# The opening of a decoder layer's kernel: split weights not kept in DRAM, the second group's x through the first one's tiles, the first weight tile in four parts, another order of splits

## The chip, the cores and the metric

One core of one Trainium2 chip runs the whole layer. The metric is the device time of one execution in microseconds; a kernel's time is the median of its runs. The kernel before takes 2134.07 us (three runs, 2131.14 to 2137.16).

## The reference

A decoder layer for 2048 tokens of 1024 features, with 16 meta tokens ahead of them. All of it is float32.

```python
xn = rms_norm(h, norm_gain[l])
proj = xn @ w_in[l]
sb_q, sb_k, sb_v, sw_q, sw_k, sw_v, sb_z, sw_z, g_sb, g_sw = jnp.split(proj, offsets, axis=-1)
o_sb = stick_breaking_attention(sb_q, sb_k, sb_v, valid)          # 8 heads of 64
q = rope(sw_q, pos); k = rope(sw_k, pos)
o_sw = sliding_window_sink_attention(q, k, sw_v, attn_sinks[l], valid)   # 16 query, 2 key heads, window 128
y_sb = (o_sb * jax.nn.silu(sb_z)) @ w_branch_sb[l]
y_sw = (o_sw * jax.nn.silu(sw_z)) @ w_branch_swa[l]
merged = jax.nn.sigmoid(g_sb) * y_sb + jax.nn.sigmoid(g_sw) * y_sw
h = h + merged @ w_out[l]
```

The shapes of heads are left out above. What matters here is the second line: one product of the normalised x with w_in, whose columns are the queries, keys, values and gates of both branches.

## The kernel before

**Split products.** TensorE multiplies operands of a narrower kind, so every float32 operand is split in two: h, its rounded copy, and l, the rest. A product is three products, h by h, l by h and h by l. `gemm` (L409 to L411) does this for one column tile of 128 columns and one group of 512 tokens: eight k slices of 128 features, three matmuls of 128x512 each, 24 in all. `gemm_meta` (L420) is the same for the 16 meta tokens, 16 small matmuls. The x operands are xh and xl, the weight operands wh and wl.

**Weights.** `weights` (L164 to L183) brings a column tile: it loads 512 KB into `raw` (two buffers), and `split` makes wh (ACT, L106, or POOL, L108) and wl (DVE or POOL, L109), with three buffers of each. It then stores both halves in DRAM (`kept`), 512 KB each, so that a later use loads wh and wl and splits nothing. In the opening these stores are collected in `put_off` and issued in two lots of six.

**Groups and halves.** The 2048 tokens are four groups of 512, worked on in two halves, groups 2 and 3 first. In the first half g0 is group 2 and g1 is group 3. The program's second half uses weight tiles that the opening had.

**The opening** (L970 to L1123) is what the change is about. ACT, SP and DVE work through its instructions in the order in which the code gives them; SP issues all DMAs. Behind it, up to `hand.close()`, DVE's order still is the code's; the rest is set by the scheduler. TensorE's order is the code's throughout. The opening goes so:

1. The first column tile, SBK0 (keys of the stick-breaking branch), and eight tiles of g0's x are loaded. x is not normalised yet: `unscaled` (L979, L980) multiplies a k slice by the gain alone and splits it. `by_halves` (L1017, L1021) splits the weight tile in two halves. Products of three column tiles (SBK0, SBQ0, SBK1; the tiles `sbt[:3]` are given in another order) run from this for g0 and g1 while the sums of squares are made.
2. Meanwhile g0's x is scaled: `normal` (L382 DVE, L383 ACT, L385 DVE) multiplies a slice by gain and row scale, casts it to xh and subtracts to xl. SWK and SWV (keys and values of the window branch) are loaded and split, and the row products of the three tiles are scaled out of PSUM (`scaled`, L1002 on DVE), then split by `evac_split` (L112 ACT, L113 DVE) and stored as kd (keys) and qd (queries), with h and l in tiles of the pool `tmp` (seven buffers).
3. g1's x is loaded a second time and scaled by `normal`. Four of its slices go to the pool `xs` (four buffers, `ring_x`), two into a buffer of `raw`, and the last two to `xs` again, which is only free when the first pair has been split. `normal` for g1 stands behind the `evac_split` of g1.

**Behind the opening** the window's products run: SWK, SWV and the first query tile SWQ0 for g0, then SWK and SWV for g1 with their meta tokens, then SWQ0 for g1 and more query tiles. `rope` (L637 to L641) turns SWK's product, with the tables ct and sn (512 KB each, one DMA each). `put_k` (L649 ACT, L651 DVE) splits it into kk, four DVE operations; `put_q` (L699) does this for queries. SWV's product is copied out (L484), turned by four transposes on TensorE (L488) into a PSUM bank, `zm`, that has one buffer, and split into vv (L112, L113).

Of the kernel before, what the change touches and what calls it, by code (L numbers as in the profile page):

```python
# [16 lines left out]
P = 128  # L17
# [4 lines left out]
GT = 512  # L22
# [17 lines left out]
def f32(ap):  # L40
    return ap.bitcast(F32)
# [3 lines left out]
def tile_kernel(ctx, tc, x, xt, meta, metat, gain, w_in, w_sb, w_sw, w_out, sinks, fgain,  # L45
# [55 lines left out]
    vsplit, hsplit = [False], [True]  # L101
# [349 lines left out]

    def low(acc):
# [517 lines left out]
    with (tc.tile_pool(name="start", bufs=1, side="left") as bp,  # L970
          tc.manual_schedule(engines={mybir.EngineType.Activation, mybir.EngineType.SP})):
        hsplit[0] = vsplit[0] = True
        raws, accs, ms = [], {}, [None] * 3

        def unscaled(g, k, t):

            DMA(t, xt[g, k])
# [37 lines left out]
        def by_halves(wh, wl, raw):  # L1015
            a, b = slice(0, KT // 2), slice(KT // 2, KT)
            A.copy(wh[:, a], raw[:, a])  # L1017
            V.tensor_tensor(wl[:, a], raw[:, a], f32(wh[:, a]), op=ALU.subtract)

            def rest():  # L1020
                A.copy(wh[:, b], raw[:, b])  # L1021
                G.tensor_tensor(wl[:, b], raw[:, b], f32(wh[:, b]), op=ALU.subtract)
            second.append(rest)
# [232 lines left out]
```

## Time and profile before

| what | value |
|---|---|
| median of three runs | 2134.07 us (2131.14 to 2137.16) |
| the profiled execution | 2136.89 us |
| its span in the trace | 2135.0 us |
| mean granted TensorE clock | 0.997 |
| DMA packets | 174519, 380.39 MB, mean 178 GB/s |
| stores of split weights | 50 of h and 50 of l, 512 KB each |
| loads of split weights | 66 of wh and 66 of wl, 512 KB each |
| loads of raw w_in tiles | 50, 512 KB each |

How to read the rows that the next sections show. Times are microseconds from the span's start. A timeline row has start, duration, engine, line, operation and tiles (out<-in), how many instructions of the kind stand together, and in brackets the idle time before with the engine or DMA that ended it. A row of waits has the engine, the tile and line that waited, whom for, and the total, the number and the longest wait. A row of windows has, for a stretch, each engine's busy time with its instruction count, then the granted clock (1.00 is full speed), the mean busy share of the 16 DMA engines and their GB/s. PE is TensorE's matmul, PEld its weight load, DVE VectorE, ACT ScalarE, POOL GpSimd, SP the queue that issues DMAs.

### The profile page before, as it was taken

To read this page: it belongs to the slowest core of one execution; us is meant where nothing else is said; L and a number is where in the kernel's file an instruction comes from. 1 tells how busy PE (TensorE), PEld (TensorE's weight loads), DVE (VectorE), ACT (ScalarE), POOL (GpSimd) and SP (SyncE) were. 2 spreads that over 40 slices of the span, in tenths; PEclk is the share of its full clock that TensorE was granted. 3 is DMA by queue.
4 is the path that set the end of the run, shared out by engine and by line. 5 is a ranking of instruction groups with operands and counts; after the bars stand their busy time and mean duration, and the time that the engine had idled before them with its cause. 6 is when DMAs were issued, how large, how long until landed. Compare 5 with 4: busy or idle time off the path is not lost.

```text
span 2135.0 us, 30157 instructions
## 1 busy us (share of the span) xinstructions
PE 2112.2 (99%) x10534; PEld 1755.9 (82%) x10534; DVE 1383.4 (65%) x2158; ACT 1030.5 (48%) x2471; POOL 333.1 (16%) x453
## 2 busy tenths in 40 slices
PE   8999999999999999999999999999999999999998
PEld 6788888888888788888888888888888888887887
DVE  7797885466555443867746888888885446553453
ACT  6677774344444434777744565555554202221121
POOL 2122332332232300122210000000000232000000
PEclk9999999999999999999999999999999999999999
DMA  9855455766556464443465333323423986557432
GB/s 334 289 182 194 173 177 175 233 219 208 183 184 204 151 221 159 157 157 139 138 196 165 121 123 118 120 97 112 119 85 132 346 297 198 192 216 270 157 110 79
DMA packets 174519, 380.39 MB, mean 178 GB/s; under 512 B 22720, under 2 KB 40960, under 8 KB 174368
## 3 DMA queue, kind: packets, MB, share of 16 engines
q1 hardware_dynamic: 174368, 378.48, 52.5%
q8 instruction: 83, 1.36, 0.3%
q14 instruction: 68, 0.56, 0.1%
HBM read 237.35 MB, written 140.98 MB: 177 GB/s over the span
## 4 chain that ended last, share of the span: by engine, by line
PE 85%; issue 7%; DMA 3%; DVE 2%; ACT 1%; SPq 1%; POOL 0%; POOLq 0%; DVEq 0%; ACTq 0%
PE ps_g L409 15%; PE ps_g L411 14%; PE ps_g L410 14%; PE ps_o L927 5%; PE ps_t L896 4%; PE ps_z L876 4%; PE ps_z L718 3%; PE ps_o L764 3%; PE ps_g L232 1%; PE ps_g L233 1%; PE ps_z L231 1%; PE ps_z L233 1%; PE ps_z L232 1%; PE ps_g L231 1%; PE ps_t L747 1%
## 5 line engine op out<-in xcount | busy, mean ns | idle before, releaser
L409 PE MATMUL ps_g<-xh,wh 128*128 128x512 f32 x1544 | 634.6, 411 | 7.0 <-ACT xh L979 7.0
L410 PE MATMUL ps_g<-xl,wh 128*128 128x512 f32 x1544 | 605.9, 392 | 0.0
L411 PE MATMUL ps_g<-xh,wl 128*128 128x512 f32 x1544 | 605.9, 392 | 0.0
L883 DVE TENSOR_TENSOR_SCAN row<-row 128x512 f32<-128x512 f32 (+2 forms) x320 | 375.6, 1175 | 157.9 <-POOL row L881 105.8
L411 PEld LDWEIGHTS ps_g<-xh,wl 128*128 128x128 f32 x1544 | 290.2, 188 | 65.5 <-DVE wl L109 0.3
L409 PEld LDWEIGHTS ps_g<-xh,wh 128*128 128x128 f32 x1544 | 291.3, 189 | 52.7 <-ACT xh L979 7.0
L410 PEld LDWEIGHTS ps_g<-xl,wh 128*128 128x128 f32 x1544 | 292.0, 189 | 43.2 <-DVE xl L980 1.3
L879 ACT ACTIVATE row<-ps_z 128x512 f32<-128x512 f32 (+2 forms) x320 | 165.0, 516 | 192.0 <-PE ps_z L876 191.3
L113 DVE SCALAR_TENSOR_TENSOR wtl<-ps_t,wth 128x512 fp32r<-128x512 f32 (+1 forms) x320 | 189.9, 594 | 55.7 <-ACT wth L112 54.9
L112 ACT ACTIVATE wth<-ps_t 128x512 fp32r<-128x512 f32 (+1 forms) x320 | 170.5, 533 | 71.8 <-PE ps_t L896 68.9
L876 PE MATMUL ps_z<-kt,q 128*128 128x512 f32 (+4 forms) x640 | 178.2, 353 | 0.0
L896 PE MATMUL ps_t<-ident,row 128*128 128x128 f32 x1088 | 171.1, 272 | 1.9 <-DVE wtl L113 1.2
L896 PEld LDWEIGHTS ps_t<-ident,row 128*128 128x128 f32 x1088 | 135.7, 140 | 39.1 <-DVE wtl L113 2.3
L881 POOL TENSOR_SCALAR_AFFINE_SELECT row<-row 128x128 f32<-128x128 f32 x128 | 42.0, 329 | 630.1 <-ACT row L879 591.0
L876 PEld LDWEIGHTS ps_z<-kt,q 128*128 128x128 f32 x640 | 118.9, 188 | 23.2
L927 PE MATMUL ps_o<-wth,vc 128*128 128x512 f32 (+1 forms) x320 | 125.1, 391 | 0.0
L108 POOL TENSOR_SCALAR wh<-raw 128x1024 fp32r<-128x1024 f32 (+1 forms) x63 | 68.2, 1082 | 336.1 <-PE ps_g L410 209.5
L726 ACT ACTIVATE sc<-sc,nm 128x129 f32<-128x129 f32 x256 | 100.2, 394 | 41.7 <-DVE nm L724 40.9
L927 PE MATMUL ps_o<-wtl,vc 128*128 128x512 f32 (+1 forms) x320 | 116.9, 365 | 0.7 <-DVE wtl L113 0.7
L577 ACT ACTIVATE tmp<-ps_g 128x512 f32<-128x512 f32 x112 | 67.0, 599 | 103.9 <-PE ps_g L411 97.5
L109 POOL TENSOR_TENSOR wl<-raw,wh 128x1024 fp32r<-128x1024 f32 (+1 forms) x43 | 100.5, 2337 | 3.3
L270 ACT CAST ringl<-gt 128x512 fp32r<-128x512 f32 x32 | 20.0, 624 | 152.3 <-DVE gt L268 144.6
(316 smaller groups left out, 3439.2 us busy)
## 6 DMA issues: line engine op xcount, KB each, us to landing
wh<-h_in_w_in SPq DMA_DIRECT2D x66, 512.0 KB, 3.6
wl<-l_in_w_in SPq DMA_DIRECT2D x66, 512.0 KB, 4.9
raw<-in_w_in SPq DMA_DIRECT2D x50, 512.0 KB, 5.1
h_in_w_in<-wh SPq DMA_DIRECT2D x50, 512.0 KB, 2.9
l_in_w_in<-wl SPq DMA_DIRECT2D x50, 512.0 KB, 2.9
q<-qd SPq DMA_DIRECT2D x128, 128.0 KB, 3.1
vc<-vd SPq DMA_DIRECT2D x48, 256.0 KB, 3.3
kd<-tmp SPq DMA_DIRECT2D x32, 256.0 KB, 3.9
```

Source lines behind the costliest of these rows:

```text
L109: (V if vsplit[0] else G).tensor_tensor(l, src, f32(h), op=ALU.subtract)
L112: A.activation(h, acc, AF.Copy, scale=scale)
L113: V.scalar_tensor_tensor(l, acc, scale, f32(h), op0=ALU.mult, op1=ALU.subtract)
L409: T.matmul(acc, lhsT=wh[:, k, :], rhs=xh[g][:, k, :], start=k == 0, stop=False)
L410: T.matmul(acc, lhsT=wh[:, k, :], rhs=xl[g][:, k, :], start=False, stop=False)
L411: T.matmul(acc, lhsT=wl[:, k, :], rhs=xh[g][:, k, :], start=False, stop=k == KT - 1)
L726: A.activation(sc[:, hh, :], sc[:, hh, :], AF.Exp, bias=nm[:, hh:hh + 1], accum_out=den[:, hh:hh + 1])
L876: T.matmul(acc[:, :b - a], lhsT=lq, rhs=kt[h][:, k0 + a:k0 + b], start=t == 0, stop=t == 1)
L879: A.activation(r[:, a:b], acc[:, :b - a], AF.Sigmoid, scale=-1.0)
L883: V.tensor_tensor_scan(r[:, :w], r[:, :w], r[:, :w], last[j] if n else 1.0, op0=ALU.mult, op1=ALU.min)
L896: T.transpose(tr[:, j * P:(j + 1) * P], rows_of[h, g, n - (j > i), j][:, k0:k0 + P], ident)
L927: T.matmul(o[:, :n], lhsT=v, rhs=r, start=first and r is wh, stop=last and r is wl)
```

## The change

It edits the opening and what goes with it:

- The six column tiles that are split in the opening (SBK0, SBQ0, SBK1, SWK, SWV, SWQ0) are no longer stored to DRAM, neither there nor later. Each later use loads the raw tile and splits it again.
- The first weight tile is loaded in four DMAs of 128 KB (two k slices each), between those of x, and split in four parts. The gain comes transposed by the host, so that a partition's eight values lie together.
- All eight slices of g1's second x are loaded, behind SWQ0's raw tile, into the eight tiles `raw0` that held g0's first x.
- `normal` for g1 stands ahead of g1's `evac_split`.
- The h halves of keys and queries go to `xs` where `spare` says that they may.

The diff, cut to its core:

```diff
-        kept[key] = [dram(f"{t}_{w.name}_{c0}", [P, n, P], F32R) for t in "hl"]
-        for t, k in zip((wh, wl), kept[key]):
-            if put_off is None:
+        if opening[0]:
+            loose.append(key)
+        elif key not in loose:
+            kept[key] = [dram(f"{t}_{w.name}_{c0}", [P, n, P], F32R) for t in "hl"]
+            for t, k in zip((wh, wl), kept[key]):
                 DMA(k, t)
-            else:
-                put_off.append((k, t))
...
+    def high():
+        return ring_x(F32R) if spare[0] else tmp(F32R)
...
-            h, l = tmp(F32R), low(acc)
+            h, l = high(), low(acc)
...
+        def by_parts(wh, wl, raw):
+            def part(a, b, e):
+                A.copy(wh[:, a:b], raw[:, a:b])
+                e.tensor_tensor(wl[:, a:b], raw[:, a:b], f32(wh[:, a:b]), op=ALU.subtract)
+            second.append(part)
...
-        raw = load(C_SBK)
-        DMA(gn, gain.rearrange("o (k p) -> p (o k)", p=P))
-        ready[C_SBK] = weights(C_SBK, raw=raw, split=by_halves)
+        DMA(*parts[0])
+        DMA(gn, gain)
+        DMA(raws[0], xt[g0, 0])
+        DMA(raws[1], xt[g0, 1])
+        for k in range(2, KT, 2):
+            DMA(*parts[k // 2])
+            for j in (k, k + 1):
+                DMA(raws[j], xt[g0, j])
+        ready[C_SBK] = weights(C_SBK, raw=raw, split=by_parts)
...
-        for k, t in put_off:
-            DMA(k, t)
-        del put_off[:]
...
-        for k in range(4):
-            new.append(ring_x())
-            DMA(new[k], xt[g1, k])
         raw = load(C_SWQ)
-        pair = wp.tile([P, KT, P], F32, tag="raw", name="raw", bufs=2).rearrange("p k c -> p (k c)")
-        for k in (4, 5):
-            new.append(pair[:, (k - 4) * GT:(k - 3) * GT])
+        for k in range(KT):
+            new.append(bp.tile([P, GT], F32, tag="raw0", name="raw0", bufs=KT))
             DMA(new[k], xt[g1, k])
...
         for n in range(3):
             outs[g1, n] = scaled(g1, n, rb1)
+        for k in range(0, KT, 2):
+            in_turns(*(normal(g1, j, new[j], rb1) for j in (k, k + 1)))
         for n in range(3):
             ts[n][1](g1, outs[g1, n], None)
...
-        for k in range(0, KT, 2):
-            in_turns(*(normal(g1, j, new[j], rb1) for j in (k, k + 1)))
-            if k == 0:
-                for j in (6, 7):
-                    new.append(ring_x())
-                    DMA(new[j], xt[g1, j])
-                for j, t in put_off:
-                    DMA(j, t)
...
-        "gain": a["norm_gain"],
+        "gain": a["norm_gain"].reshape(KT, P).T,
```

Lines move a little: L382, L383 and L385 become L385, L386 and L388; L409 to L411 become L412 to L414; L420 becomes L423, L427 L430, L488 L495, L639 to L641 become L646 to L648, L649 and L651 become L656 and L658, L699 L706, and L1002 L1010.

TensorE's instructions stand in the same order as before. On DVE, before, from the scaling of the last unscaled product on (ps_t; L113 are the splits of g1's keys and queries, L382 and L385 are `normal` of g1):

```order
L1002 TENSOR_TENSOR tmp<-ps_t,rb 128x512
L113 SCALAR_TENSOR_TENSOR tmp<-tmp 128x512 x3
L382 SCALAR_TENSOR_TENSOR xs<-xs,gn,rb 128x512 x2
L385 TENSOR_TENSOR xl<-xs,xh 128x512 x2
L382 SCALAR_TENSOR_TENSOR xs<-xs,gn,rb 128x512 x2
L385 TENSOR_TENSOR xl<-xs,xh 128x512 x2
```

And now, at the same place (raw_733 and so on are the `raw0` tiles with g1's x; the pairs of 737, 739, 741 and 743 between are of the same form):

```order
L1010 TENSOR_TENSOR tmp<-ps_t,rb 128x512
L385 SCALAR_TENSOR_TENSOR raw_733<-raw_733,gn,rb 128x512
L385 SCALAR_TENSOR_TENSOR raw_735<-raw_735,gn,rb 128x512
L388 TENSOR_TENSOR xl<-raw_733,xh 128x512
L388 TENSOR_TENSOR xl<-raw_735,xh 128x512
...
L388 TENSOR_TENSOR xl<-raw_745,xh 128x512
L388 TENSOR_TENSOR xl<-raw_747,xh 128x512
L113 SCALAR_TENSOR_TENSOR tmp<-tmp,xs 128x512 x3
```

The three splits have moved behind the four pairs. Next on DVE, before, the rope of SWK for g0 and g1, up to the split of the first transposes of SWV:

```order
L639 SCALAR_TENSOR_TENSOR tmp<-ps_g,ct 128x512
L640 TENSOR_TENSOR tmp<-tmp,sn 128x512
L641 TENSOR_TENSOR tmp<-tmp 128x512
L639 SCALAR_TENSOR_TENSOR tmp<-ps_z,ct 128x512
L640 TENSOR_TENSOR tmp<-tmp,sn 128x512
L641 TENSOR_TENSOR tmp<-tmp 128x512
L651 TENSOR_TENSOR kk<-tmp,kk 64x512 x4
L699 TENSOR_TENSOR q<-tmp,q 64x512 x2
L113 SCALAR_TENSOR_TENSOR vv<-ps_zm,vv 128x8x64
```

(ps_g is SWK's product for g0, ps_z SWQ0's.) And now:

```order
L646 SCALAR_TENSOR_TENSOR tmp<-ps_g,ct 128x512
L109 TENSOR_TENSOR wl<-raw,wh 128x1024
L647 TENSOR_TENSOR tmp<-tmp,sn 128x512
L648 TENSOR_TENSOR tmp<-tmp 128x512
L646 SCALAR_TENSOR_TENSOR tmp<-ps_z,ct 128x512
L647 TENSOR_TENSOR tmp<-tmp,sn 128x512
L648 TENSOR_TENSOR tmp<-tmp 128x512
L658 TENSOR_TENSOR kk<-tmp,kk 64x512 x4
L109 TENSOR_TENSOR wl<-raw,wh 128x1024
L706 TENSOR_TENSOR q<-tmp,q 64x512 x2
L113 SCALAR_TENSOR_TENSOR vv<-ps_zm,vv 128x8x64
```

Two weight splits have come in between: that of the next value tile, and the second one of SWQ0. On SP's queue, before, around the tables (ct, sn; kd_2 and kd_3 are keys of g0 and g1, the number behind it names the tile):

```order
L55 DMA kd_2_101<-tmp 128x512 x2
L55 DMA ct<-in_cost 128x1024
L55 DMA sn<-in_sint 128x1024
L55 DMA raw<-in_w_in 128x1024
L55 DMA kd_3_98<-tmp 128x512 x2
L55 DMA qd_3_82<-tmp 128x512 x2
L55 DMA kd_3_102<-tmp 128x512 x2
```

And now (h_in_w_in is the store of a split half of a query tile that is kept):

```order
L55 DMA kd_2_101<-tmp 128x512
L55 DMA raw<-in_w_in 128x1024
L55 DMA h_in_w_in_1074<-wh 128x1024
L55 DMA kd_3_98<-xs 128x512
L55 DMA ct<-in_cost 128x1024
L55 DMA kd_3_98<-tmp 128x512
L55 DMA qd_3_82<-xs 128x512
L55 DMA qd_3_82<-tmp 128x512
L55 DMA kd_3_102<-xs 128x512
L55 DMA kd_3_102<-tmp 128x512
L55 DMA msd_288<-ms 16x128
L55 DMA sn<-in_sint 128x1024
```

ct and sn have moved behind a raw tile, a store of a split half and the stores of g1's keys and queries, and no longer stand together.

More of the change, by code (lines that the diff above doesn't have):

```diff
@@ L99, in tile_kernel @@
     vsv = dram("vsv", [P, 2 * P], F32R)
-    vsplit, hsplit = [False], [True]
+    vsplit, hsplit, opening = [False], [True], [True]
     def split(h, l, src):
@@ L156, in tile_kernel, with load @@
     kept = {}
-    put_off, ready = [], {}
-    def load(c0, w=w_in):
+    loose, ready = [], {}
+    def load(c0, w=w_in, parts=None):
         raw = wp.tile([P, KT, P], F32, tag="raw", name="raw", bufs=2)[:, :w.shape[2], :]
-        DMA(raw, w[c0 // P])
+        if parts is None:
+            DMA(raw, w[c0 // P])
+        else:
+            parts.extend((raw[:, a:a + 2], w[c0 // P][:, a:a + 2]) for a in range(0, KT, 2))
         return raw
@@ L474, in use @@
         def use(g, acc, ms):
-            h, l = tmp(F32R), low(acc)
+            h, l = high(), low(acc)
             evac_split(h, l, acc, 0.125)
@@ L972, in tile_kernel, with unscaled @@
         hsplit[0] = vsplit[0] = True
-        raws, accs, ms = [], {}, [None] * 3
-        def unscaled(g, k, t):
-            DMA(t, xt[g, k])
+        accs, ms = {}, [None] * 3
+        def unscaled(g, k, t, loaded=False):
+            if not loaded:
+                DMA(t, xt[g, k])
             uh, ul = xh["u", g][:, k, :], xl["u", g][:, k, :]
@@ L1013, in tile_kernel @@
         second = []
[L1015 to L1023, printed above, removed]
-        raw = load(C_SBK)
-        DMA(gn, gain.rearrange("o (k p) -> p (o k)", p=P))
-        ready[C_SBK] = weights(C_SBK, raw=raw, split=by_halves)
+        def by_parts(wh, wl, raw):
[3 more added lines that the diff above has]
+            second.append(part)
+        parts = []
+        raw = load(C_SBK, parts=parts)
+        raws = [bp.tile([P, GT], F32, tag="raw0", name="raw0", bufs=KT) for k in range(KT)]
+        DMA(*parts[0])
[7 more added lines that the diff above has]
+        ready[C_SBK] = weights(C_SBK, raw=raw, split=by_parts)
         ts = [sbt[0]()]
         x_tiles(("u", g0), 1)
+        part = second[0]
+        part(0, 2, V)
         for k in range(KT):
-            raws.append(bp.tile([P, GT], F32, tag="raw0", name="raw0", bufs=KT))
-            unscaled(g0, k, raws[k])
-            if k == 0:
-                second[0]()
+            unscaled(g0, k, raws[k], True)
+            if k % 2 and k < KT - 1:
+                part(k + 1, k + 3, G)
         ts.append(sbt[2]())
@@ L1115, in tile_kernel @@
             DMA(msd[n // 2], ms[n])
-        for k in range(0, KT, 2):
-            in_turns(*(normal(g1, j, new[j], rb1) for j in (k, k + 1)))
-            if k == 0:
-                for j in (6, 7):
-                    new.append(ring_x())
-                    DMA(new[j], xt[g1, j])
-                for j, t in put_off:
-                    DMA(j, t)
-    put_off = None
+    opening[0] = False
     held = pending[:]
```

## The prediction

> **What bounds the kernel now.** I read the page first, then TensorE's waits in the first 200 us, then its timeline with the granted clock at the places where it waited.
>
> ```profile
> PE 2112.2 (99%) x10534; PEld 1755.9 (82%) x10534; DVE 1383.4 (65%) x2158; ACT 1030.5 (48%) x2471; POOL 333.1 (16%) x453
> PE 85%; issue 7%; DMA 3%; DVE 2%; ACT 1%; SPq 1%; POOL 0%; POOLq 0%; DVEq 0%; ACTq 0%
> ```
>
> TensorE is busy 99% of the span and makes 85% of the chain that ends last. The change gives it the same matmuls in the same order, so only its idle time and the clock granted to it can move the end. In the opening there is not much idle time to win:
>
> ```profile
> PE ps_g L409 <- ACT xh L979: 7.0, 1, 7.0
> PE ps_o L409 <- ACT xh L383: 1.6, 1, 1.6
> PE ps_zm L527 <- DVE vt L113: 0.5, 1, 0.5
> PE ps_o L410 <- DVE xl L385: 0.4, 2, 0.2
> ```
>
> The 7.0 us lie before the first matmul. The second and fourth lines are one place: SWK's product for the second group g1, which waits for the halves of g1's scaled x. What that place costs in all is seen in TensorE's timeline (start, duration; the bracket is idle time and who ended it) and in the windows:
>
> ```profile
> 7.01 0.79 PE L409 MATMUL ps_g<-xh,wh 128*128 128x512 f32 x1 [7.01 <-ACT xh L979]
> ...
> 11.64 0.39 PE L409 MATMUL ps_g<-xh,wh 128*128 128x512 f32 x1
> ...
> 15.06 0.39 PE L409 MATMUL ps_g<-xh,wh 128*128 128x512 f32 x1
> ...
> 64.91 0.40 PE L409 MATMUL ps_o<-xh,wh 128*128 128x512 f32 x1
> ...
> 68.53 0.50 PE L409 MATMUL ps_o<-xh,wh 128*128 128x512 f32 x1 [1.59 <-ACT xh L383]
> ...
> 73.50 0.45 PE L409 MATMUL ps_z<-xh,wh 128*128 128x512 f32 x1
> ...
> 79.01 0.22 PE L420 MATMUL ps_t<-wh,mx 128*48 128x128 f32 x1
> ...
> 79.97 0.45 PE L409 MATMUL ps_g<-xh,wh 128*128 128x512 f32 x1
> ...
> 84.80 0.60 PE L488 MATMUL ps_zm<-ident,tmp 128*128 128x128 f32 x4
> ```
>
> ```profile
> 66.06:69.47 3.41, 1.59 (x6) 0.72 (x5) 2.45 (x5) 1.54 (x3) 0.00 (x0) 1.00 1.02 407
> 69.50:70.00 0.50, 0.50 (x2) 0.26 (x2) 0.50 (x2) 0.47 (x2) 0.00 (x0) 0.50 1.01 401
> 73.00:73.50 0.50, 0.50 (x12) 0.50 (x10) 0.49 (x1) 0.49 (x2) 0.00 (x0) 1.00 1.02 410
> ```
>
> (The last three columns are granted clock, DMA share and GB/s.) At full speed a product's 24 matmuls take 79.01 - 73.50 = 5.51 us, 0.23 each, and the 16 small ones for the meta tokens 79.97 - 79.01 = 0.96. Between 64.91 and 73.50 stand 12 of the first, the 16 of the second and four transposes. That is 2.76 + 0.96, and about 0.4 for the transposes, an estimate from their 0.60 with the overlap of neighbours taken off: 4.1 of the 8.59 us. So this place loses **4.5 us**: 1.6 + 0.4 of waiting, and the rest through the clock, which was at 0.50 at 69.5 and back at 1.00 at 73.0, after TensorE had been busy 1.59 of 3.41 us. DMA is full throughout (share 1.02).
>
> **The change part by part.** *The stall at 65 to 73.* DVE and DMA make it:
>
> ```profile
> 52.02 0.69 DVE L1002 TENSOR_TENSOR tmp<-ps_o,rb 128x512 f32<-128x512 f32 x1 [1.23 <-DMA kd<-tmp]
> 53.92 0.69 DVE L1002 TENSOR_TENSOR tmp<-ps_t,rb 128x512 f32<-128x512 f32 x1 [1.21 <-DMA kd<-tmp]
> ...
> 60.64 1.41 DVE L382 SCALAR_TENSOR_TENSOR xs<-xs,gn,rb 128x512 f32<-128x512 f32 x2
> ...
> 63.34 1.41 DVE L382 SCALAR_TENSOR_TENSOR raw<-raw,gn,rb 128x512 f32<-128x512 f32 x2
> ...
> 67.08 1.41 DVE L382 SCALAR_TENSOR_TENSOR xs<-xs,gn,rb 128x512 f32<-128x512 f32 x2 [0.94 <-DMA xs<-in_xt]
> ```
>
> A pair of k slices takes 63.34 - 60.64 = 2.70 us on DVE, and the last pair began at 67.08 only because its x came late. In the changed kernel all eight slices of g1's x are loaded before the stores of k and q, into the tiles of the first x, and the pairs stand directly behind the last L1010. The h halves of k and q go to the xs ring, so the two waits for stores out of tmp (1.23 and 1.21) should go: the last scaling ends at 53.92 + 0.69 - 2.44 = 52.2, and the four pairs at 52.2 + 4 x 2.70 = **63.0**. TensorE was at the fifth slice of SWK's product at 64.91 and takes 0.69 us for a slice, so it needs the last pair near 64.91 + 2 x 0.69 = 66.3. Slack 3 us; with both tmp waits kept the pairs end at 65.4 and still are in time. The 4.5 us go.
>
> *The wait that comes in.* The tables ct and sn of SWK's rope were issued one behind the other:
>
> ```profile
> 53.22 0.61 SPq L55 DMA_DIRECT2D sn<-in_sint  x1
> h_in_w_in<-wh SPq DMA_DIRECT2D x50, 512.0 KB, 2.9
> ```
>
> That is 16 us before DVE used them. Now ct lies in memory that the last pair (63.0) still uses, behind a raw tile, the store of a split half and a store of k; five 256 KB stores and sn follow, and sn waits for ct's landing. At 0.40 MB/us (the 401 to 410 GB/s above), 0.5 + 0.5 + 0.25 + 0.5 MB from 63.2 on put ct's landing at 67.6; 1.3 MB of stores and 0.5 of sn put sn's at **72.2**. Both ends: 69.5, if half of the transfers in front have landed by 63, and 76, if SP's queue stands still for each. I take 72.2, since DMA is full in the rows on both sides. Behind sn DVE has, in order:
>
> ```profile
> 73.53 0.69 DVE L641 TENSOR_TENSOR tmp<-tmp 128x512 f32<-128x512 f32 x1
> 74.68 5.95 DVE L651 TENSOR_TENSOR kk<-tmp,kk 64x512 fp32r<-64x512 f32 x4 [0.46 <-ACT kk L649]
> 80.66 1.41 DVE L699 TENSOR_TENSOR q<-tmp,q 64x512 fp32r<-64x512 f32 x2
> 82.10 0.69 DVE L113 SCALAR_TENSOR_TENSOR vv<-ps_zm,vv 128x512 fp32r<-128x512 f32 x1
> ...
> 86.60 2.79 DVE L651 TENSOR_TENSOR kk<-tmp,kk 64x512 fp32r<-64x512 f32 x4 [0.69 <-ACT kk L649]
> ```
>
> ```profile
> 73.69 1.44 POOL L108 TENSOR_SCALAR wh<-raw 128x1024 fp32r<-128x1024 f32 x1 [19.58 <-PE ps_t L420]
> 75.22 2.71 POOL L109 TENSOR_TENSOR wl<-raw,wh 128x1024 fp32r<-128x1024 f32 x1
> ```
>
> ```profile
> 14.29 1.23 DVE L109 TENSOR_TENSOR wl<-raw,wh 128x1024 fp32r<-128x1024 f32 x1 [0.89 <-ACT wh L106]
> ```
>
> Five rope operations at 0.67 are 3.35; 0.46 for ACT's cast; the four kk operations 2.79 alone and 5.95 beside POOL's split, of which only one wh of 1.44 is beside them now: 3.5; one wl, SWQ0's second split, 1.23; q 1.41; vv 0.69. Together 10.64, so vv ends at 72.2 + 10.6 = **82.8**. Queued behind it on TensorE are the second four transposes (84.80 in the row above), because their PSUM bank has one buffer and vv empties it. They would otherwise be due at 84.80 - 4.5 - 0.5 (the start, below) = 79.8: a wait of **3.0 us**, between 0 (sn at 69) and 7 (sn at 76). It eats most of the gain: the transposes come at 82.8, 2.0 before where they stood. The wait of 1.59 us brought the clock to 0.50 for 3.4 us, 1.7 us lost. I take the same once: **-2.0 + 1.7 = -0.3 us**.
>
> [...]
>
> *The start.*
>
> ```profile
> 6.23 0.72 ACT L979 ACTIVATE xh<-raw,gn 128x512 fp32r<-128x512 f32 x1 [1.08 <-DMA raw<-in_xt]
> ...
> 13.21 1.05 ACT L106 CAST wh<-raw 128x1024 fp32r<-128x1024 f32 x1 [1.21 <-DMA raw<-in_w_in]
> ```
>
> ```profile
> 3.00:3.50 0.50, 0.00 (x0) 0.00 (x0) 0.00 (x0) 0.00 (x0) 0.50 (x2) 1.00 1.01 393
> 4.00:4.50 0.50, 0.00 (x0) 0.00 (x0) 0.00 (x0) 0.00 (x0) 0.23 (x1) 1.00 1.06 96
> ```
>
> The gains' 1024 pieces hold the DMA engines at 96 GB/s for half a microsecond; now each partition has one piece of 32 bytes. Of the weight tile 128 KB instead of 512 lie ahead of the first x: 0.38 MB at 0.393 MB/us is 1.0 us. With 0.5 for the gains the first matmul comes at about 5.4 instead of 7.01. But the same 3 MB lie ahead of the second product's raw tile, so its wh (13.21) and wl (14.29) come only 0.5 earlier, and TensorE, which had come to that product at 15.06 and to its third matmul before the wl was done (15.52), now comes there earlier and waits 1 us longer. So 0.5 of 1.6 us is kept. Bounds: 1.6, if that tile comes sooner too; 1.2 lost, if the longer gap keeps the clock down (nine matmuls took 4.63 us to 11.64 where 15 took 3.42 to 15.06: 2.6 us of cold start, and half of it again). Where the wait at 80 comes, it swallows this, since SP and DVE set that.
>
> [...] The trace moved 393 GB/s in 256 KB transfers; of 128 KB parts no row here shows a rate.
>
> *The stores and second splits.* Twelve stores of 512 KB leave the queue (the row of 512 KB above), 6 MB or 15 us of full DMA, that nobody waited for at the time. In the second half each of the six tiles is read raw (512 KB for 1024) and split again: 1.44 on POOL, 1.23 on DVE.
>
> ```profile
> 767.54 1.42 DVE L382 SCALAR_TENSOR_TENSOR xs<-xs,gn,rb 128x512 f32<-128x512 f32 x2 [1.05 <-DMA xs<-in_xt]
> ...
> 777.35 1.36 DVE L385 TENSOR_TENSOR xl<-xs,xh 128x512 fp32r<-128x512 f32 x2
> ```
>
> Here DVE waits over 1 us for x ahead of a pair, and 1.23 fits in such gaps, with less to load. I cost it at nothing; without that cover three splits of 1.23 stand before 778.7, where TensorE uses the last pair as it comes: 0 to 3.7 us.
>
> **The rivals.** *No new wait* (0.17): sn lands before 69.5. For it: 6 MB of stores are gone; against: the transfers in front remain. Gain 4.5 + 0.5 = 5.0: 2129.1; with all of the start 2128. [...] *Tables late* (0.13), on the slower side: the tmp waits stay (ct 2.4 us later) and POOL stretches kk to 5.95 (2.4 more), so vv ends at 87.6, 2.8 behind the old place of the transposes, with 1.7 to 3.4 for the clock: +4.5 to +6.2, 2139 to 2140.3. It is slower than before from vv ending after 83.1. *Second splits uncovered* (0.08): -0.3 + 2.5, 2136. *The stall stays* (0.04), since DVE's pairs come after 66 in spite of the new order: 0.5 gained, 2133.6.
>
> **How the numbers follow.** The forecast has 0.44. The profiled execution took 2136.89 us, 2135.0 of it span; -0.3 gives 2136.6 there, and from the runs' median of 2134.07, 2.8 lower, **2133.8**. Its own range is 2131.5 to 2136. For eight in ten the range takes in nearly all of the first rival and the lower part of tables late: 2128.5 to 2139. A measurement here can tell about 0.3% (6.4 us) from no change, and the runs of before lie 6 us apart. Below 2127.7 lies only the first rival with luck at the start (0.08), above 2140.5 tables late with a second drop, or uncovered splits on top (0.07); 0.85 lies between.
>
> **What would show it.** Right: first matmul near 5.4 and a gap of 1 to 2 us before L414 at 13 to 15; no wait of ps_o for xh or xl near 65; DVE's L647 waiting for sn to about 72; ps_zm at L495 waiting about 3 us for vv near 80, and the clock at 0.5 for some 3.4 us behind it; no wait of TensorE at the second half's start. Wrong: sn landed before 69; no clock below 1 after the wait; L413 waiting for xl near 66; a wait at 770 to 790 for L385 or L109.

## The result and the profile after

The changed kernel takes **2147.42 us** (median of four runs, 2144.86 to 2148.66) against 2134.32 of the kernel before (four runs on the same chip, 2131.14 to 2137.16): ratio 1.006, 95% interval 1.0043 to 1.0078. It is slower, by about 13 us, and lies above the forecast's range. Its profiled execution took 2147.04 us, 2145.3 of it span, 10.3 more than before's 2135.0. One execution of a kernel below, of the one with two pools, ran at a granted clock of 0.85 throughout (2327.07 us) and is left out of its median.

TensorE's waits name the places at once (waiter, whom for, total, number, longest):

```profile
PE ps_g L412 <- ACT xh L987: 5.5, 1, 5.5
PE ps_zm L495 <- DVE vv L113: 4.8, 1, 4.8
PE ps_g L414 <- DVE wl L109: 2.7, 2, 2.1
...
PE ps_zm L495 <- ACT tmp L491: 1.5, 1, 1.5
...
PE ps_o L413 <- DVE xl L388: 1.1, 1, 1.1
```

The same waits stand in TensorE's timeline:

```profile
5.47 0.79 PE L412 MATMUL ps_g<-xh,wh 128*128 128x512 f32 x1 [5.47 <-ACT xh L987]
...
15.78 0.50 PE L414 MATMUL ps_g<-xh,wl 128*128 128x512 f32 x1 [0.53 <-DVE wl L109]
...
66.47 0.39 PE L412 MATMUL ps_o<-xh,wh 128*128 128x512 f32 x1
68.00 0.51 PE L413 MATMUL ps_o<-xl,wh 128*128 128x512 f32 x1 [1.14 <-DVE xl L388]
...
70.23 1.12 PE L495 MATMUL ps_zm<-ident,tmp 128*128 128x128 f32 x4 [1.50 <-ACT tmp L491]
...
90.08 0.72 PE L495 MATMUL ps_zm<-ident,tmp 128*128 128x128 f32 x4 [4.79 <-DVE vv L113]
...
860.52 0.50 PE L414 MATMUL ps_g<-xh,wl 128*128 128x512 f32 x1 [2.14 <-DVE wl L109]
```

TensorE runs the same instructions in the same order in both kernels, so each can be laid beside its twin; an *offset* below is its start here minus its start before. The first matmul is 1.5 us earlier (5.47 against 7.01), and at L414 of the second product this is used up (15.78 against 15.57: +0.2). At the matmul that waited 1.59 us before (68.53, now 66.47) the offset is -2.1, and the old stall seems gone. But the very next matmul waits for xl, and the first transposes for ACT's copy. At 70.23 the offset is +0.1. The second transposes stand at 90.08 instead of 84.80: **+5.3**. Half clock behind them makes it +6.9 at 94.44, and small steps 8.0 at 360. In the second half the offset is 8.3 at 857.98; then 860.52 stands against 849.91 (+10.6), and half clock makes that **+12.2** at 865.08. About 2 us come back later, 1.3 of them near 1940, and the end is at +10.3. The row of before:

```profile
849.91 0.39 PE L411 MATMUL ps_g<-xh,wl 128*128 128x512 f32 x1
```

So there are two places: 6.9 us in the opening, and 3.9 (8.3 to 12.2) at 858 to 865. The windows show the clock behind each wait (busy time of PE, PEld, DVE, ACT and POOL, granted clock, DMA share, GB/s):

```profile
60.00:64.00 4.00, 4.00 (x20) 3.30 (x19) 3.98 (x6) 1.25 (x2) 1.52 (x1) 1.00 0.01 3
...
68.00:72.00 4.00, 2.50 (x9) 1.88 (x10) 2.50 (x4) 3.92 (x8) 2.04 (x6) 0.75 0.60 156
...
92.00:96.00 4.00, 4.00 (x15) 3.21 (x14) 2.22 (x5) 3.79 (x7) 0.00 (x0) 0.76 0.72 262
...
863.00:866.00 3.00, 3.00 (x10) 2.40 (x9) 0.00 (x0) 0.00 (x0) 0.00 (x0) 0.61 1.02 399
```

From 60 to 64, in the first row, DMA moved 3 GB/s. Before, it was full there:

```profile
60.00:64.00 4.00, 4.00 (x20) 3.30 (x18) 3.97 (x7) 1.25 (x2) 0.00 (x0) 1.00 0.99 381
```

Something held the queue.

**What made the pairs and the tables late.** DVE's timeline of the opening:

```profile
49.03 4.13 DVE L113 SCALAR_TENSOR_TENSOR tmp<-tmp,xs 128x512 fp32r<-128x512 f32 x3
...
54.89 1.40 DVE L385 SCALAR_TENSOR_TENSOR raw<-raw,gn,rb 128x512 f32<-128x512 f32 x2
...
63.01 4.33 DVE L385 SCALAR_TENSOR_TENSOR raw<-raw,gn,rb 128x512 f32<-128x512 f32 x2
67.27 1.45 DVE L388 TENSOR_TENSOR xl<-raw,xh 128x512 fp32r<-128x512 f32 x2
68.63 1.89 DVE L113 SCALAR_TENSOR_TENSOR tmp<-tmp,xs 128x512 fp32r<-128x512 f32 x3
73.46 0.69 DVE L646 SCALAR_TENSOR_TENSOR tmp<-ps_g,ct 128x512 f32<-128x512 f32 x1 [2.94 <-DMA ct<-in_cost]
...
79.66 0.69 DVE L647 TENSOR_TENSOR tmp<-tmp,sn 128x512 f32<-128x512 f32 x1 [3.32 <-DMA sn<-in_sint]
...
89.24 0.69 DVE L113 SCALAR_TENSOR_TENSOR vv<-ps_zm,vv 128x512 fp32r<-128x512 f32 x1
```

Beside it POOL's:

```profile
49.31 2.71 POOL L109 TENSOR_TENSOR wl<-raw,wh 128x1024 fp32r<-128x1024 f32 x1
62.48 1.52 POOL L108 TENSOR_SCALAR wh<-raw 128x1024 fp32r<-128x1024 f32 x1 [10.46 <-PE ps_z L413]
64.09 2.71 POOL L109 TENSOR_TENSOR wl<-raw,wh 128x1024 fp32r<-128x1024 f32 x1
68.78 0.52 POOL L635 MEMSET kk<- 128x512 f32 x1 [1.98 <-DVE xl L388]
```

Two rows of DVE are far too long: three splits took 4.13 where three take 1.89 at 68.63, and the last pair's two scalings 4.33 where the first pair's took 1.40. Each lies over a weight split of POOL. Together they hold the pairs back by 2.2 + 2.9 us: the last xl ends at 68.7 and not near 63. The first transposes wait on top of that, because ACT now has g1's three key and query splits between the last xh and the copy for the transposes, which starts at 69.59:

```profile
67.90 1.66 ACT L112 ACTIVATE xs<-tmp 128x512 fp32r<-128x512 f32 x3
```

Before, the copy followed the last xh at once.

SP's queue:

```profile
64.03 0.32 SPq L55 DMA_DIRECT2D h_in_w_in<-wh  x1
68.55 0.32 SPq L55 DMA_DIRECT2D kd<-xs  x1
68.98 0.37 SPq L55 DMA_DIRECT2D ct<-in_cost  x1
...
72.89 1.30 SPq L55 DMA_DIRECT2D msd<-ms  x2
74.24 0.43 SPq L55 DMA_DIRECT2D sn<-in_sint  x1
```

SP stood until 64.03 for POOL's wh, until 68.55 for ACT's split of a key, and ct left at 68.98, 0.26 us after the last xl. Five stores of 256 KB and the msd stores stand between it and sn, which left at 74.24 and landed at 79.6.

**The second half.** DVE, then POOL:

```profile
857.94 0.69 DVE L113 SCALAR_TENSOR_TENSOR vt<-ps_zm,vt 128x512 fp32r<-128x512 f32 x1 [3.72 <-ACT vt L112]
...
859.24 1.22 DVE L109 TENSOR_TENSOR wl<-raw,wh 128x1024 fp32r<-128x1024 f32 x1
```

```profile
841.76 1.04 POOL L108 TENSOR_SCALAR wh<-raw 128x1024 fp32r<-128x1024 f32 x1 [27.87 <-DVE vv L113]
```

This is SWQ0's tile for the second half's second group, split again because its halves are no longer in DRAM. Its wh was ready at 842.8. Its wl stands on DVE behind the split of vt, for which DVE waited idle until 857.94, so it ended at 860.46 and TensorE waited 2.14 us for it.

### The profile page after: what moved, and what is told of

Its sections match the earlier page's. It is cut to its first block, busy times and chain, and to the rows that moved or that the text cites. A ratio compares the mean times of both kernels' runs of the same rounds, so it can differ in the third digit from the quotient of the medians.

```text
span 2145.3 us, 30163 instructions
## 1 busy us (share of the span) xinstructions
PE 2115.5 (99%) x10534; PEld 1758.7 (82%) x10534; DVE 1394.4 (65%) x2166; ACT 1029.5 (48%) x2473; POOL 344.7 (16%) x463
## 4 chain that ended last, share of the span: by engine, by line
PE 80%; issue 9%; DVE 6%; DMA 3%; ACT 2%; POOL 0%; SPq 0%; POOLq 0%; DVEq 0%; ACTq 0%
PE ps_g L412 13%; PE ps_g L414 13%; PE ps_g L413 13%; PE ps_o L934 5%; PE ps_t L903 4%; PE ps_z L883 4%; PE ps_z L725 2%; PE ps_o L771 2%; PE ps_g L235 1%; PE ps_g L236 1%; PE ps_g L234 1%; PE ps_z L235 1%; PE ps_z L236 1%; PE ps_z L234 1%; PE ps_t L235 1%
## 5 line engine op out<-in xcount | busy, mean ns | idle before, releaser
L412 PE MATMUL ps_g<-xh,wh 128*128 128x512 f32 x1544 | 637.1, 413 | 5.5 <-ACT xh L987 5.5
L414 PE MATMUL ps_g<-xh,wl 128*128 128x512 f32 x1544 | 608.0, 394 | 2.7 <-DVE wl L109 2.7
L414 PEld LDWEIGHTS ps_g<-xh,wl 128*128 128x128 f32 x1544 | 291.3, 189 | 68.7 <-DVE wl L109 3.5
L412 PEld LDWEIGHTS ps_g<-xh,wh 128*128 128x128 f32 x1544 | 292.6, 189 | 52.0 <-ACT xh L987 6.0
L113 DVE SCALAR_TENSOR_TENSOR wtl<-ps_t,wth 128x512 fp32r<-128x512 f32 (+1 forms) x320 | 189.8, 593 | 55.1 <-ACT wth L112 54.4
L108 POOL TENSOR_SCALAR wh<-raw 128x1024 fp32r<-128x1024 f32 (+1 forms) x71 | 78.0, 1099 | 425.4 <-PE ps_g L413 191.0
```

The lines of the kernel that those rows point to most:

```text
L113: V.scalar_tensor_tensor(l, acc, scale, f32(h), op0=ALU.mult, op1=ALU.subtract)
L412: T.matmul(acc, lhsT=wh[:, k, :], rhs=xh[g][:, k, :], start=k == 0, stop=False)
L414: T.matmul(acc, lhsT=wl[:, k, :], rhs=xh[g][:, k, :], start=False, stop=k == KT - 1)
```

## The experiments

Three theories, named in the expectations below. **A**: the tables ct and sn are late, because they wait for the opening's memory (g1's second x lies in it) and because SP works through its queue in order. **B**: SWQ0's halves are not kept, and its second split stands on DVE in the way of the second half. **C**: POOL's splits beside DVE slow DVE, which keeps the old stall alive. The rivals are that not keeping six tiles is the whole loss, that the order of splits is, and that the new start is. All edits are to the changed kernel, but for the start alone. Each kernel is compared with runs of the kernel before on the same chip, whose median was 2132.9 to 2134.0. Against its own, the changed kernel is 13.1 us above (2147.42 - 2134.32); for the experiments that told most the same difference is given.

**No sine table in the first half** (the cosine table stands in its place, so a part of the rotation is changed).

```diff
-        DMA(sn, sint[:, groups[0] * GT:(groups[0] + 2) * GT])
+        if half == 0:
+            sn = ct
+        else:
+            DMA(sn, sint[:, groups[0] * GT:(groups[0] + 2) * GT])
```

> In the first half the sine table is not loaded and the cosine table stands in its place (part of the rope is wrong by that). Theory A, late tables: in the changed kernel sn lands at 79.6 us, DVE's rope waits for it, the split vv ends at 89.9 and TensorE's second transposes wait 4.8 us; without sn the rope can go on behind ct and the value tile's split at 76.3, so vv ends near 86.6, the wait falls to 1.5 us or so, and the span by 3 to 5 us. Rival, DVE's own work (the extra weight splits and kk) sets vv: the wait stays at 4 to 5 us and the time is that of the changed kernel.

Measured: 2144.55 us, ratio 1.005 (1.0035 to 1.0065). The wait for vv falls from 4.8 to 0.2, and the offset at 95.86 is +3.1 instead of +6.9. So the wait at 90 does hang on sn's landing. The waits at 67 to 72 and the one at 858 are untouched, and the end is at +8.4.

**SWQ0's first split in the second half on POOL.**

```diff
-                drain(tiles_by_tile([sw_k, sw_v], groups), tiles_by_tile(q[0], groups[:1]))
+                drain(tiles_by_tile([sw_k, sw_v], groups))
+                vsplit[0] = False
+                drain(tiles_by_tile(q[0][:1], groups[:1]))
+                vsplit[0] = True
+                drain(tiles_by_tile(q[0][1:], groups[:1]))
```

> In the second half the l half of SWQ0's second split is made by POOL, not by DVE. Theory B, place in DVE's queue: in the changed kernel this split stands on DVE behind a split of vt that waits for TensorE, and TensorE then waits 2.1 us for it at 860 and runs at half clock behind; on POOL it is done some 10 us before, the wait and the half clock go, and the time falls by 4 us (2143). Rival, the second split is late because its raw tile or wh is late: the wait stays and the time is unchanged.

Measured: 2148.29, ratio 1.0073 (1.0056 to 1.0089). The wait at 859.3 stays at 2.14. This moved the wrong split: SWQ0 is split twice in the second half, once for each group, and it is the second that TensorE waits for.

**SWQ0 kept in DRAM**, its stores at the opening's end.

```diff
-        if opening[0]:
+        if opening[0] and not (c0 == C_SWQ):
             loose.append(key)
+        elif opening[0]:
+            kept[key] = [dram(f"{t}_{w.name}_{c0}", [P, n, P], F32R) for t in "hl"]
+            put_off.extend(zip(kept[key], (wh, wl)))
...
+        for k, t in put_off:
+            DMA(k, t)
```

> SWQ0's halves are kept in DRAM again (stored at the end of the opening), the other five tiles are not. Theory B: the 4 us at 860 go, since SWQ0's halves are loaded there. In the opening the second split of SWQ0 leaves DVE's queue (1.2 us ahead of vv), but two more stores of 512 KB go through the full queue, so vv ends between 1.2 us earlier and 1.5 later. Sum -3 to -6: 2142 to 2144. Rival, that all six second splits cost: only a sixth to a third goes, 2 to 4 us, and the wait at 860 stays in part.

Measured: 2141.42, ratio 1.0038 (1.0023 to 1.0053): 8.2 above before instead of 13.1, so 4.9 less, for one tile kept. In its trace TensorE has no wait at 845 to 866. What is left is in the opening:

```profile
87.78 1.08 PE L498 MATMUL ps_zm<-ident,tmp 128*128 128x128 f32 x4 [5.88 <-DVE vv L113]
```

The offset is +3.0 there, +4.6 behind the half clock and +4.0 at the end. B holds. But not all of the gain is in the second half: 2.3 us of it are in the opening (+4.6 instead of +6.9), where DVE has no second split of SWQ0 (1.23) between sn and vv any more and its four kk operations take 2.78 instead of 3.62. One thing was not intended: POOL splits the next query tile at 70.63, behind the pairs, so that each of the four pairs takes 2.7 us, the last xl ends at 66.8 and the stall at 65 to 73 is gone. Since sn is used as late as in the changed kernel (79.44), all that the pairs gain is waited for at the second transposes.

**All six tiles kept** (the condition above is always true, with a first lot of stores ahead of g1's first x).

> All six tiles are kept in DRAM again, six stores behind SWV's raw tile and six at the end of the opening, as before; the rest of the change stays. Theory B: the 4 us at 860 go. Theory A: the tables are still behind the stores of g1, and six more stores lie ahead of or beside them, so the wait at 90 stays at 4 to 7 us: 2142 to 2146. Rival, that not keeping the tiles is the whole loss: the time comes back to 2134 or, with the stall at 65 gone, to 2130.

Measured: 2146.11, ratio 1.0062 (1.0047 to 1.0077). The second half has no stall, but sn leaves at 77.91 behind the stores, the wait for vv is 8.7 and the second transposes stand at 93.48 (+8.7). So not keeping the tiles isn't the whole loss: six stores of kept halves, issued from 72.49 on, stand ahead of sn, which leaves 3.7 us later than in the changed kernel (74.24). The rival falls.

**g1's splits of keys and queries ahead of `normal` again.**

```diff
-        for k in range(0, KT, 2):
-            in_turns(*(normal(g1, j, new[j], rb1) for j in (k, k + 1)))
         for n in range(3):
             ts[n][1](g1, outs[g1, n], None)
         spare[0] = False
+        for k in range(0, KT, 2):
+            in_turns(*(normal(g1, j, new[j], rb1) for j in (k, k + 1)))
```

> Only the order of splits is as before: g1's keys and queries are split and stored ahead of g1's scaled x. Theory A (tables late, because the opening's tiles are held until the last slice of x): the pairs move back by the 1.9 us of the three splits, so the stall at 66 grows by about 2; ct and sn now stand together, but still behind the last pair, so sn lands at 74 to 76 instead of 79.6 and vv's wait falls by some 4. Sum between -3 and 0: 2144 to 2148. Rival, that the order of splits is the loss: the time comes back to 2138 to 2141.

Measured: 2145.9, ratio 1.0057 (1.004 to 1.0074). TensorE waits 3.0 us for xl at 67.23 (+3.5), the wait for vv is 0.7 and the second transposes come at 88.59 (+3.8); a wait of 1.54 for DVE's tmp makes that +5.6 at 98.28. The order moves the stall from the tables to the pairs; it isn't the cause of the loss. This run also shows ct with no store of g1 ahead of it: SP issues nothing from 67.5 on, and ct leaves when the last xl ends (73.19).

```profile
71.83 1.36 DVE L388 TENSOR_TENSOR xl<-raw,xh 128x512 fp32r<-128x512 f32 x2
```

```profile
73.25 0.33 SPq L55 DMA_DIRECT2D ct<-in_cost  x1
```

**g1's second x where it was before** (four slices in `xs`, two in a raw buffer, two in `xs` again; h halves in `tmp`).

```diff
+        for k in range(4):
+            new.append(ring_x())
+            DMA(new[k], xt[g1, k])
         raw = load(C_SWQ)
-        for k in range(KT):
-            new.append(bp.tile([P, GT], F32, tag="raw0", name="raw0", bufs=KT))
+        pair = wp.tile([P, KT, P], F32, tag="raw", name="raw", bufs=2).rearrange("p k c -> p (k c)")
+        for k in (4, 5):
+            new.append(pair[:, (k - 4) * GT:(k - 3) * GT])
             DMA(new[k], xt[g1, k])
```

> Only the places of g1's second x are as before (four slices in xs, two in raw, the last two in xs when the first pair is split; the h halves in tmp again); the order of splits and the unkept tiles stay as changed. Theory A: the opening's tiles are free early, ct and sn land before 62, vv's wait at 85 goes to 0 to 1.5 us; the last pair waits for its x as before, so some of the stall at 65 comes back; the 4 us in the second half stay. Sum: 2136 to 2140. Rival, that the extra splits on DVE and POOL set the opening: the wait for vv stays at 3 us or more and the time above 2143.

Measured: 2144.76, ratio 1.0059 (1.0039 to 1.0079), above what theory A gave. ct leaves at 55.03 and sn at 55.43, and there is no wait for vv: the use of the `raw0` tiles is what holds the tables. But the last pair's scalings take 3.54 beside POOL's split, and the first transposes wait:

```profile
73.96 1.11 PE L495 MATMUL ps_zm<-ident,tmp 128*128 128x128 f32 x4 [4.49 <-ACT tmp L491]
```

That is +3.9, and the stall at 858 is there as well. POOL's split accounts for at most 2.9 us of this wait (2.1 on those scalings, 0.8 on the xl ahead of them). The rest is ACT: its four rope operations on SWK's product, done at 51.7 to 54.1 in the changed kernel, stand here at 70.22 to 72.61, behind the splits of g1 and ahead of the copy that the transposes need:

```profile
73.32 0.59 ACT L491 COPY tmp<-ps_g 128x512 f32<-128x512 f32 x1 [0.71 <-DVE tmp L646]
```

So A alone doesn't carry the opening, but this run moves more than A, and how much of what is left is C it doesn't show.

**g1's stores of keys and queries behind the tables.**

```diff
+    def store(dst, src, g):
+        if spare[0] and g == 3:
+            put_by.append((dst, src))
+        else:
+            DMA(dst, src)
...
             sw_k, sw_v, sw_q, attend, ending = window(half, groups, sp)
+            for d, t in put_by:
+                DMA(d, t)
```

> All of the change stays; g1's stores of keys and queries are issued behind the tables, so that sn follows ct at once. Theory A: ct still comes behind the last pair (69), sn lands near 72 instead of 79.6, vv ends near 83, and TensorE's wait of 4.8 us at 90 and the half clock behind it go; the two stalls that remain are that near 68 and that in the second half. Sum -5 to -6: 2141.5 to 2142.5. Rival, DVE's own work: vv's wait stays over 2 us, time above 2144.

Measured: 2144.5, ratio 1.005 (1.0035 to 1.0065). sn leaves at 71.13, 0.43 behind ct, and the wait for vv at the second transposes is gone. The waits at 69 to 72 stay (+2.2 behind them), and two short ones for DVE (0.2 and 0.8) make the offset +3.6 at 96.34. ct itself still leaves only at 70.70, so of A the stores in between make about 3 us at this place, and what holds ct is untouched.

**Both second-half splits of SWQ0 on POOL.**

```diff
+            def on_pool(p):
+                v, vsplit[0] = vsplit[0], vsplit[0] and m
+                r = sw_q(p)
+                vsplit[0] = v
+                return r
```

> In the second half both further splits of SWQ0 have their l half on POOL (the run with SWQ0's first one there did not touch the one that TensorE waited for, which is for the second group). Theory B: the wait of 2.1 us at 860 and the half clock behind it go, -4 us: 2143.5. Rival, that wh or the raw tile is late there: the wait stays, only with POOL's name.

Measured: 2147.17, ratio 1.0068 (1.0053 to 1.0083): no gain. DVE's wl isn't waited for any more, but DMA is, on TensorE:

```profile
864.25 0.47 PE L412 MATMUL ps_g<-xh,wh 128*128 128x512 f32 x1 [1.05 <-DMA wh<-h_in_w_in]
...
866.74 0.50 PE L414 MATMUL ps_g<-xh,wl 128*128 128x512 f32 x1 [1.79 <-DMA wl<-l_in_w_in]
```

and on SP's queue:

```profile
858.04 0.66 SPq L55 DMA_DIRECT2D vd<-vt  x1
858.80 1.73 SPq L55 DMA_DIRECT2D wh<-h_in_w_in  x2
```

SP had stood for 23.0 us ahead of the vd store, which needs vt (split by 858.0), with the loads of the next halves behind it; before, the same loads left at 849.40 and 855.34, each ahead of its store. TensorE reached the place at +7.7 and is at +10.8 at 911. So B has two limbs, the split on DVE and the order on SP, and taking away the one uncovers the other.

**The next query tile's wl (SWQ1) on DVE instead of POOL.**

```diff
-                vsplit[0] = False
                 drain(tiles_by_tile(q[0][1:], groups[:1]))
-                vsplit[0] = True
```

> All of the change stays; only the l half of SWQ1's split (the second query tile) is made by DVE and not by POOL, which in the changed kernel works from 64.1 to 66.8 beside DVE's last pair. Theory C, POOL slows DVE: the last pair's two scalings took 4.33 us there and 1.41 elsewhere; now they take 1.4 and DVE pays 1.23 for the split, so the last slice of x, and with it ct and sn, come 1.7 us earlier, and the stall near 68 and the wait at 90 shrink together by 1.5 to 3: 2144 to 2146. Rival, that the last pair waited for something else: it still takes 4 us, and the 1.23 come on top, 2148.5.

Measured: 2147.67, ratio 1.0062 (1.0047 to 1.0077). DVE:

```profile
64.48 1.41 DVE L385 SCALAR_TENSOR_TENSOR raw<-raw,gn,rb 128x512 f32<-128x512 f32 x2
65.81 1.21 DVE L109 TENSOR_TENSOR wl<-raw,wh 128x1024 fp32r<-128x1024 f32 x1
```

The last pair's scalings are 1.41 again instead of 4.33, which shows C's mechanism. But the split now stands in DVE's own order, the last xl ends at 68.2 instead of 68.7, and the tables are as late as ever (sn is used at 79.58, wait for vv 6.5). Alone it is worth nothing.

**Three at once**: SWQ0 kept, the stores behind the tables, SWQ1's wl on DVE.

> The change with three edits together: SWQ0 is kept in DRAM, g1's stores are issued behind the tables, and SWQ1's l half is made by DVE. If theories A, B and C hold and add up, the opening loses 4 to 6 us less and the second half 4: 2147.4 - 8 to -10, which is 2137 to 2139, and if the stall of before at 65 to 73 is really gone, down to 2133. Rival, that the new order of DVE itself costs (kk and rope all fall behind the pairs): vv's wait is replaced by waits of ps_g for DVE's tmp, and the time stays at 2140 or above.

Measured: 2139.15 (eight runs), ratio 1.0024 (1.0014 to 1.0034). The stall at 65 to 73 is nearly gone (0.5 and 0.4 of waiting), but ct leaves at 68.22 and the second transposes still wait:

```profile
84.76 1.09 PE L505 MATMUL ps_zm<-ident,tmp 128*128 128x128 f32 x4 [2.93 <-DVE vv L113]
```

They stand where they stood before, and half clock follows (matmuls begin 0.43 us apart from 86.07 to 87.35, and 0.23 from 87.99 on): the end is at +4.0.

**The start alone**, put into the kernel before (gain from the host, first tile in four parts).

> The kernel before with only the new start: the first weight tile in four parts, and the transposed gain. The prediction gave this 0.5 us. By the changed kernel's trace the first matmul comes 1.5 us earlier and the second product's third matmul no earlier (15.78 for 15.57): so the same time, 2133 to 2135. Rival, that the start is a part of the loss (the clock stays down longer, the second product's tile comes later): 2136 or more.

Measured: 2135.87 (ten runs), ratio 1.001 (1.0000 to 1.0020). The first matmul is 1.0 us earlier, L414 of the second product 0.9 later. The start gains nothing. By the medians this kernel is 2.3 us above before, at the edge of the interval, so this run alone doesn't exclude that the start is a small part of the loss; the last experiment speaks against it.

**The `raw0` tiles in a pool of their own, the window's pool in two**, so that ct and sn don't wait for g1's second x; nothing else of the change undone.

```diff
+    early = ExitStack()
+    fp = early.enter_context(tc.tile_pool(name="first", bufs=1, side="right"))
...
-            new.append(bp.tile([P, GT], F32, tag="raw0", name="raw0", bufs=KT))
+            new.append(fp.tile([P, GT], F32, tag="raw0", name="raw0", bufs=KT))
...
+        early.close()
+        sq = second.enter_context(tc.tile_pool(name=f"swb{half}", bufs=1, side="left"))
```

> All of the change stays, and nothing is computed otherwise; the tiles of g1's second x lie in a pool of their own, at the other end of memory, and the window's pool is cut in two, so that its first part (kk, vv, ct, sn, q) can start when the opening's other tiles are free. Theory A (the tables are late because the opening's pool is held until the last slice of g1's x): ct and sn land before 62 instead of 73.4 and 79.6, DVE goes on with the rope behind its splits at 70.5, vv ends near 81, and the wait of 4.8 us at 90 and the half clock behind it go: 2141 to 2142. Rival, that DVE's own work or the new order of splits sets vv: tables early, but vv still later than 85 and a wait of over 2 us, 2145 or more.

Measured: 2141.45 (three runs, 2138.35 to 2145.26), ratio 1.0041 (1.0026 to 1.0057): 8.6 above before instead of 13.1, so 4.5 less. No row of this kernel is shown; that its tables go early is seen in the next kernel, which has the same pools.

**The same, with SWQ0 kept and SWQ1's wl on DVE.**

> The run with two pools, and SWQ0 kept in DRAM, and SWQ1's l half on DVE. If the three causes add up: the opening about 3 us shorter than before at 84 (the stall at 65 to 73 gone, as in the run with three edits, and no new wait), nothing lost in the second half: 2131 to 2133, 1 to 3 below the kernel before. Rival, that what is won in the opening is given back behind it (the clock, or later waits for DVE): 2134 to 2137.

Measured: 2133.63 (eleven runs), ratio 1.0001 (0.9992 to 1.001), 0.8 above before by the medians, which the runs can't tell from nothing. The loss is gone. On SP:

```profile
50.40 0.34 SPq L55 DMA_DIRECT2D ct<-in_cost  x1
51.40 0.33 SPq L55 DMA_DIRECT2D sn<-in_sint  x1
```

and on DVE:

```profile
63.46 1.41 DVE L388 SCALAR_TENSOR_TENSOR raw<-raw,gn,rb 128x512 f32<-128x512 f32 x2
...
66.16 1.89 DVE L113 SCALAR_TENSOR_TENSOR tmp<-tmp,xs 128x512 fp32r<-128x512 f32 x3
67.97 0.69 DVE L651 SCALAR_TENSOR_TENSOR tmp<-ps_g,ct 128x512 f32<-128x512 f32 x1
...
79.94 0.69 DVE L113 SCALAR_TENSOR_TENSOR vv<-ps_zm,vv 128x512 fp32r<-128x512 f32 x1
```

The tables leave 19 and 23 us earlier, the rope starts at 67.97 without a wait, and vv ends at 80.6 instead of 89.9. The only wait that TensorE's timeline shows between 60 and 110 is one of 0.31, and at 68.96 the offset is -3.3: the gain that the opening could give is there. It is -2.7 at 774, and half of that goes at 787, where TensorE waits for a split on DVE that stands among the scalings of x (DVE itself had waited 1.93 us for x at 783):

```profile
786.99 0.50 PE L415 MATMUL ps_g<-xh,wh 128*128 128x512 f32 x1 [1.21 <-DVE tmp L113]
```

The end is at -1.4. POOL's split of SWQ1 starts at 70.12 here, behind the pairs, as in the run that keeps SWQ0 alone. So these runs show that the three edits together are enough, and not how much the third adds to the other two.

**The same with the old start.**

> The same with the start of the kernel before (the first weight tile in one transfer, the gain in small pieces). If the new start is worth nothing, as the trace of the run with the start alone has it, the same time within 1 us; if it is worth the 0.5 us of the prediction, or 1.5, this one is slower by that.

Measured: 2133.92 (eleven runs), ratio 1.0003 (0.9995 to 1.0012). The old start does no worse.

## Why the prediction was wrong

**The step that failed is "the wait that comes in", at its first number: sn landed at 79.6, not at 72.2.** Two things were taken wrongly there. The end of the pairs, 63.0, was 68.7: the waits for tmp went as forecast, three pairs took 2.70 each as forecast, but POOL's splits added 2.2 to the key splits and 2.9 to the last pair. The end of the pairs makes 5.7 of the 7.4 us. And the queue was costed by bytes at 0.40 MB/us, "since DMA is full in the rows on both sides"; in the event DMA moved 3 GB/s from 60 to 64, because SP stood for a split and then for the pairs. From the end of the pairs to ct's landing at 73.4 it still came out near the forecast (4.7 us for 4.6). Behind ct, where SP issued the stores in order, 6.2 us passed to sn's landing for 4.6: the other 1.6.

**The reason given for ct was right in effect.** With nothing else ahead of it ct left 0.06 us after the last xl (73.25, in the run with the order back), and it left early in the two runs shown in which the last pair no longer held it: at 55.03 with g1's x where it was before, and at 50.40 with a pool of their own for the `raw0` tiles. It isn't ct alone that waits: POOL's memset of kk stands for the last xl as well (68.78, above). Whether the bytes of ct are those of a `raw0` tile, as the forecast says, or the opening's memory is handed on as a whole, no run shows.

**From sn on, the sum was right.** From 79.6 to vv's end at 89.93 it took 10.3 us; forecast was 10.6. The half clock behind the wait cost 1.6 (+5.3 to +6.9); forecast was 1.7. The wait of 2.14 us at 860.52 too was followed by a clock of 0.61 from 863 to 866. But the step from a wait to the half clock, which the forecast took over from one row, isn't certain: in four of the experiments the same wait of 2.14 us at the same matmul left the clock at 1.00.

**The stall of 4.5 us did not go**, against the forecast's best-founded term: TensorE came to the pairs at 66.9 with the last one still 1.8 us from done. That is the rival called *the stall stays*, for which 0.04 was given, and its cause was in the quoted rows: the forecast itself read that POOL's split stretched kk from 2.79 to 5.95, but it asked only which split would lie over kk, not which would lie over the pairs. The size of the term was nearly right: in the best kernel, where the pairs are in time, the same place gains 3.9 us (from +0.3 at 64.34 to -3.6 at 69.92).

**The second splits were costed at nothing and cost 3.9 us** in the profiled execution (2.9 to 3.2 in those four of the experiments in which the clock stayed up), at the upper end of the 0 to 3.7 allowed, and elsewhere than looked at: not DVE's gap ahead of 778.7, but the tile that is needed again by the second group at 858. "A gap of over 1 us, and 1.23 fits" is true of DVE's sum and says nothing of its order: DVE was idle for 3.72 us right ahead of 857.94, with the wh of that split ready for 15 us, and waited for something else.

**The start was right in kind**: 5.47 against 5.4 forecast, and used up by the second product. One row was misread for it: the 393 GB/s before were those of the 512 KB weight tile (packets of 4096 bytes) and not of 256 KB transfers. With parts of 128 KB among the x, the changed kernel moved 393 and 397 GB/s from 3.5 to 4.5, but 29 from 2.5 to 3.0. *Tables late* was the rival nearest to what came, with vv at 87.6 (it was 89.9) and 2139 to 2140.3. With the second splits' 3.9 it gives some 2144, and nothing on the list put the two together.

The sum of the parts, as the runs show them: one tile kept takes 4.9 us off, the tables let go early take 4.5 off, and both with SWQ1's l half on DVE take 12.3 of the 13.1 off. What stays open is the cause of the 1.1 us between 94 and 360, and why the best kernel, 3.6 us ahead at 70 and 1.4 ahead at its end, is no faster than before by the medians; both were only read from traces.

## What to carry to other kernels

When a buffer is reused for longer, ask what the next stage's first loads wait for: here the tables were held until the reused buffers were done with (ct left at 68.98, 0.26 us after the last xl), and sn, behind them in SP's order, was held too, until 74.24. Price a moved DMA by what stands ahead of it and when that may leave, not by bytes at the full rate. Work that "fits into a gap" fits only if it stands ahead of the wait that makes the gap, in that engine's order.

## What the runs showed of the hardware

- **In three places a DVE operation ended only behind the POOL operation beside it.** In the changed kernel POOL's wh ran to 64.00 and its wl to 66.80. The first scaling of the last pair, begun at 63.01, ended at 64.54, and the second at 67.34, each 0.54 us behind POOL's operation; with POOL idle a scaling takes 0.75.

```profile
64.46 2.88 DVE L385 SCALAR_TENSOR_TENSOR raw<-raw,gn,rb 128x512 f32<-128x512 f32 x1
```

  One of the three splits that took 4.13 instead of 1.89 shows the same beside the wl that ended at 52.02: it ended at 52.57. Not every DVE operation beside a split was held: an xl of the third pair, begun at 62.40, 0.08 ahead of the wh that ended at 64.00, took 0.69. Which are held, and why, these runs don't show.
- **Behind a wait of 2.14 us TensorE's clock was halved in some runs and stayed up in others.** Waits of 2.14 us (at 860.52) and 2.93 us (with three edits, at 84.76) were each followed by some 3 us at half clock (0.50 from 862 to 865 in the changed kernel), which cost 1.6 and 1.4 us beside the wait. But in four runs (no sine table, SWQ0's first split on POOL, the order back, g1's stores later) the wait of 2.14 us at the same matmul left the clock at 1.00. With SWQ0's first split on POOL the matmul started at 859.34, and the window as far behind it as 863 to 866 is in the changed kernel reads:

```profile
862.00:865.00 3.00, 3.00 (x17) 2.51 (x16) 0.00 (x0) 0.58 (x1) 0.00 (x0) 1.00 1.01 397
```

  So the length of a wait alone doesn't decide it; what does, these runs don't show. A wait of 1.21 (786.99 in the best kernel) left the clock at 1.00 too: the matmuls behind it took 0.40.
